# Modulation columns placed behind the MLP's output tiles, the beginning's columns in free slots, the first low halves on VectorE

## The chip, the cores and the metric

The kernel runs on one core of a Trainium2 chip. The metric is the device time of one execution in microseconds (us); the number given is the median of several runs. A core has five engines that each work through their own instructions in order and wait for each other by semaphores: TensorE (PE; its weight loads are the rows PEld), VectorE (DVE), ScalarE (ACT), GpSimd (POOL) and SyncE (SP), whose queue issues all the transfers between main memory and the on-chip memory here. TensorE's results land in PSUM, in banks of 128x512 numbers; everything else lies in SBUF.

## The reference

The program is a decoder trunk of two layers on 512 positions of width 1024, float32 throughout. Each layer has a mixer (an mLSTM of four heads beside a convolution with 31 taps) and a squared-ReLU MLP, and both are modulated by numbers that depend on the vector `c` alone:

```python
c_act = jax.nn.silu(c)
for l in range(DEPTH):                       # DEPTH = 2
    mod = c_act @ w_ada[l] + b_ada[l]        # 1024 -> 6 * 1024
    sh_mix, sc_mix, gt_mix, sh_mlp, sc_mlp, gt_mlp = split(mod, 6)

    h = rms_norm(x, g_pre_mix[l]) * (1 + sc_mix) + sh_mix
    y = mixer(h, ...)                        # w_in, conv, q/k/v, heads, w_out
    x = x + gt_mix * rms_norm(y, g_post_mix[l])

    h = rms_norm(x, g_pre_mlp[l]) * (1 + sc_mlp) + sh_mlp
    f = square(relu(h @ w_ff1[l])) @ w_ff2[l]     # 1024 -> 4096 -> 1024
    x = x + gt_mlp * rms_norm(f, g_post_mlp[l])
```

The change concerns `mod`: 6 x 1024 numbers for each layer, 48 columns of 128, and a weight matrix of 24 MB for each layer that is read once.

## The kernel before

Activations lie with the channels on the 128 partitions and the 512 positions along the row, so x is eight tiles of 128x512. Every large product is computed in three passes of a rounded format (lines 172 to 178): weights and activations are each split into a high half (rounded) and a low half (the rest), and a product is high x high + high x low + low x high. A block of weights of 128x1024 is therefore fetched by SP into one of four `raw` tiles, ScalarE writes its high half (L168) and GpSimd its low half (L169), into two `whi` and two `wlo` tiles, or, where a block is prepared early, into tiles of the pool `slot`, which has 25 (`wblock`, L157). A tile of a product takes 24 passes for each block and ends in one of three `ps_mm` banks.

The modulation is computed in two ways:

- `ada_rows` (L230) on TensorE, for 40 of layer 0's 48 columns, four columns a call: four blocks of 128x1024 of `in_wadn` are fetched into the three `adr` tiles in turn, multiplied by `c` (L239), copied to SBUF (L242), turned to columns by four small products (L244), and VectorE adds the bias (L250, L252). The calls 0 and 2, then 1 and 3, stand at the program's beginning, since the first `h` needs them; the calls 4 to 9 stand among the mixer's steps.
- `ada_col` (L256) on VectorE, for the last 8 columns of layer 0 and the 48 of layer 1: a block of 128x1024 of `in_wadt` is fetched into an `adr` tile and one instruction (L263) multiplies it by the broadcast `c` and sums along the row. The 56 calls stand in the code of layer 0's MLP, one behind each output tile of the first matrix from the eighth on, two behind each of the second (`some`, L280).

The order in which an engine gets its instructions is not that of the code. A scheduler walks through a simulated timeline and places an instruction as early as its inputs, its buffers and its engine are free, weights with a priority ahead of the rest. `behind(later, earlier)` (L105) adds no wait on the chip; it only says that `later` must not be placed ahead of `earlier`.

The beginning (L794 to L813): x comes in, its row sums are formed, the calls 0 and 2 give shift and scale of the first four channel tiles, `make_h` (L333) forms their h with a multiply on VectorE (L338), the high half on ScalarE (L344) and the low half on VectorE (L345), and the same with calls 1 and 3 for the other four. The first six output tiles (`glu_start`, L453) are accumulated side by side in six banks over the eight channel tiles, with weights `in_win0` of 128x768 for each, whose halves lie in slots; the first four channel tiles are called the first half below, the others the second half.

The mixer follows a list of steps (`ORDERS`, L66). The convolution (L416) runs on VectorE as 31 multiply-adds for each of eight channel groups. The heads come in three steps: `head_a` (scores, L649, weighted by VectorE, L651), `head_b` (numerator, L661; then on VectorE statistics L667 and L668, small vectors L670 to L676, a power on GpSimd L146, L679, and the scaling L681) and `head_c` (transposes on TensorE, L690, and the output gate L692, whose halves are split on ScalarE and GpSimd). Between them lie tiles of the output projection (L743). The MLP forms 2 x 16 tiles of the first matrix, each evicted by `f_out` (L753: ScalarE, VectorE L756, ScalarE, VectorE L758), and 2 x 8 tiles of the second, copied by ScalarE (L784) or added by VectorE (L787); `finish` (L347) does the last part of each product with norm and residual.

Of the kernel before, what the change touches and what calls it, by code (L numbers as in the profile page):

```python
# [10 lines left out]
F32 = mybir.dt.float32  # L11
F32R = mybir.dt.float32r
AF = mybir.ActivationFunctionType
ALU = mybir.AluOpType
# [39 lines left out]
def trunk(ctx, tc, xT, vecs, bg, cst, ccol, crow, wadn, wadt, win, win0, wqkv, wgate, wout, wff1, wff2, yT):  # L54
# [174 lines left out]

    def ada_rows(nb, tag):  # L230

        bk = bank(tag)
        for kk in range(NF // 2):
            raw = wpool.tile([P, D], F32, name="adr", tag="adr", bufs=ADR)
            sp.dma_start(out=raw, in_=wadn[nb, kk])
            for j in range(2):
                k = 2 * kk + j
                g = k % 4
                pe.matmul(bk[32 * g:32 * g + 32, :], cc[:, k:k + 1].broadcast_to([P, 32]), raw[:, j * T:(j + 1) * T],  # L239
                          start=(k < 4), stop=(k >= 4), skip_group_check=True)  # L240
# [12 lines left out]

    late = []

    def ada_col(l, c):  # L256

        one, gain = ADA[c // 8]
        scale = 1.0 if gain is None else vec(gain, l)[:, c % 8:c % 8 + 1]
        raw = wpool.tile([P, D], F32, name="adr", tag="adr", bufs=ADR)  # L260
        sp.dma_start(out=raw, in_=wadt[l, c])
        m, ini = mods[l][:, c:c + 1], inits[l][:, c:c + 1]
        dve.tensor_tensor_reduce(raw, raw, cbc, scale, 0.0 if one else ini, ALU.mult, ALU.add, m)  # L263
        if one:
            late.append((l, c))
# [486 lines left out]
    def mlp(l, hp, pre):  # L752
        def f_out(o, pr, ts):  # L753
            rl = scr.tile([P, T], F32, name="rl", tag="rl", bufs=3)
            act.activation(out=rl[:, ts], in_=o, func=AF.Relu)  # L755
            dve.tensor_tensor(o, rl[:, ts], o, op=ALU.mult)  # L756
            act.copy(out=r32(pr[:, 0, ts]), in_=o)  # L757
            dve.tensor_tensor(r32(pr[:, 1, ts]), o, pr[:, 0, ts], op=ALU.subtract)  # L758

        y = None  # L760
        for hf in range(2):
# [19 lines left out]
            for m in range(NF):  # L781
                o = gemm([wff2[l, hf, m, k] for k in range(2 - hf)], fp)
                if hf == 0:
                    act.copy(out=y[m], in_=o)  # L784
                    some(2)
                else:
                    dve.tensor_tensor(y[m], y[m], o, op=ALU.add)  # L787
                    some(2)
# [18 lines left out]
    for hf in range(2):  # L807
        ada_rows(hf, "ax" if hf else "mm")
        ada_rows(2 + hf, "ax" if hf else "mm")
        for i in range(4 * hf, 4 * hf + 4):  # L810
            pre[i] = wblock(win0[i], slot, pri=0)
            hp.append(slot())
# [72 lines left out]
```

## Time and profile before

| | |
|---|---|
| median of 3 runs | 1661.32 us (1660.44 to 1661.95) |
| the profiled execution | 1659.15 us, of it 1657.2 us in the span of the trace |
| TensorE busy | 1568.1 us (95%), 8076 matmuls |
| VectorE busy | 877.9 us (53%) |
| ScalarE busy | 712.7 us (43%) |
| GpSimd busy | 836.0 us (50%) |
| transfers | 188.91 MB, 114 GB/s over the span |

The profile is one execution of the kernel. A row of the timeline gives start, duration, engine, line, operation, the tiles written and read, and in brackets how long the engine had been idle before and what ended that idle time. A row of the table by stretches gives for each engine the busy time and the number of instructions, then the mean clock granted to TensorE (1 is full speed, and it falls to 0.5), the busy share of the DMA engines and what they moved. The row of a group has count, total and mean time. Busy time on TensorE includes work at a lowered clock.

### The profile page before, as it was taken

What the parts mean: (1) busy time and instruction counts of PE and PEld (TensorE: products, weight loads), DVE (VectorE), ACT (ScalarE), POOL (GpSimd) and SP (SyncE); (2) the same over time, 40 slices, a digit from 0 to 9 for tenths busy, and PEclk for the clock granted to TensorE, in tenths of its full rate; (3) what the DMA queues carried; (4) which work ended last, traced back from release to release, by engine and by line L of the source; (5) the groups of instructions that cost most, each with busy time, mean ns of one, the idle gap of its engine ahead of it and who ended that gap; (6) DMA issues with size and microseconds to landing.
All of it is one profiled execution on the core that took longest, in us unless ns stands there. A gap on an engine that the chain in (4) does not pass through costs nothing.

```text
span 1657.2 us, 21339 instructions
## 1 busy us (share of the span) xinstructions
PE 1568.1 (95%) x8076; PEld 1271.7 (77%) x8076; DVE 877.9 (53%) x1685; ACT 712.7 (43%) x1242; POOL 836.0 (50%) x502
## 2 busy tenths in 40 slices
PE   5999989977899999999999999899999999999997
PEld 2677766655699888888899877577789888888887
DVE  2599999799855320022126999988424520012214
ACT  3245664523255432233345367544455432233332
POOL 2557663226584444444555587533585344444462
PEclk7999999988999999999999999999999999999999
DMA  7424333576752232232432022221143132323341
GB/s 282 168 83 139 104 113 127 176 252 217 273 173 63 90 91 100 89 102 89 128 127 84 26 83 81 85 73 55 39 140 103 43 111 89 101 90 96 95 127 52
DMA packets 56270, 188.91 MB, mean 114 GB/s; under 512 B 6376, under 2 KB 8552, under 8 KB 56168
## 3 DMA queue, kind: packets, MB, share of 16 engines
q1 hardware_dynamic: 56168, 187.56, 34.4%
q8 instruction: 63, 1.03, 0.3%
q14 instruction: 39, 0.32, 0.1%
HBM read 185.44 MB, written 2.10 MB: 113 GB/s over the span
## 4 chain that ended last, share of the span: by engine, by line
PE 66%; DVE 12%; POOL 2%; issue 2%; ACT 1%; DMA 1%; POOLq 0%; ACTq 0%; DVEq 0%
PE ps_mm L176 20%; PE ps_mm L177 20%; PE ps_mm L178 20%; DVE ps_cv L416 5%; DVE adr L263 2%; PE ps_mm L661 1%; PE ps_mm L649 1%; DMA adr<-in_wadt 1%; PE ps_ax L303 1%; POOL slot L169 1%; DVE small L477 0%; POOL yt L169 0%; DVE slot L681 0%; ACT whi L168 0%; POOL wlo L169 0%
## 5 line engine op out<-in xcount | busy, mean ns | idle before, releaser
L169 POOL TENSOR_TENSOR wlo<-raw,whi 128x1024 fp32r<-128x1024 f32 (+1 forms) x216 | 499.7, 2314 | 546.8 <-ACT whi L168 518.6
L176 PE MATMUL ps_mm<-slot,whi 128*128 128x512 f32 (+1 forms) x1632 | 626.1, 384 | 10.9 <-ACT slot L154 5.6
L178 PE MATMUL ps_mm<-slot,wlo 128*128 128x512 f32 (+1 forms) x1632 | 623.4, 383 | 1.7 <-POOL wlo L169 1.2
L177 PE MATMUL ps_mm<-slot,whi 128*128 128x512 f32 (+1 forms) x1632 | 624.7, 383 | 0.1
L168 ACT CAST whi<-raw 128x1024 fp32r<-128x1024 f32 (+1 forms) x216 | 216.4, 1002 | 495.4 <-PE ps_mm L177 348.6
L176 PEld LDWEIGHTS ps_mm<-slot,whi 128*128 128x128 f32 x1632 | 309.7, 190 | 80.5 <-ACT slot L154 6.5
L178 PEld LDWEIGHTS ps_mm<-slot,wlo 128*128 128x128 f32 x1632 | 309.7, 190 | 71.8 <-issue 6.2
L177 PEld LDWEIGHTS ps_mm<-slot,whi 128*128 128x128 f32 x1632 | 310.0, 190 | 66.6 <-issue 3.8
L416 DVE SCALAR_TENSOR_TENSOR ps_cv<-slot,vv,ps_cv 128x512 f32<-128x512 f32 x480 | 334.0, 746 | 2.2
L756 DVE TENSOR_TENSOR ps_mm<-rl,ps_mm 128x512 f32<-128x512 f32 (+1 forms) x78 | 46.7, 599 | 390.3 <-ACT rl L755 390.3
L176 PE MATMUL ps_mm<-slot 128*128 128x256 f32 (+1 forms) x568 | 160.5, 293 | 10.1 <-DVE slot L758 7.4
L177 PE MATMUL ps_mm<-slot 128*128 128x256 f32 (+1 forms) x568 | 163.4, 291 | 0.3 <-DVE slot L345 0.3
L178 PE MATMUL ps_mm<-slot 128*128 128x256 f32 (+1 forms) x568 | 162.6, 290 | 0.0
L169 POOL TENSOR_TENSOR slot<-raw,slot 128x1024 fp32r<-128x1024 f32 (+1 forms) x42 | 101.3, 2429 | 58.4 <-ACT slot L168 21.0
L176 PEld LDWEIGHTS ps_mm<-slot 128*128 128x128 f32 x568 | 106.6, 192 | 14.3 <-DVE slot L758 8.3
L177 PEld LDWEIGHTS ps_mm<-slot 128*128 128x128 f32 x568 | 108.5, 191 | 3.5 <-DVE slot L345 1.0
L178 PEld LDWEIGHTS ps_mm<-slot 128*128 128x128 f32 x568 | 108.6, 192 | 1.1
L146 POOL TENSOR_TENSOR small<-small,mhalf 128x4 f32<-128x4 f32 (+1 forms) x38 | 37.4, 983 | 81.8 <-DVE small L145 80.2
L263 DVE CUSTOM_DVE_ANT_0 adr<-adr,cbc,ini 128x1024 f32<-128x1024 f32 x40 | 67.6, 1697 | 8.2 <-DMA adr<-in_wadt 8.2
L519 POOL TENSOR_TENSOR xa<-xa,s 128x512 f32<-128x512 f32 x48 | 62.2, 1295 | 8.9 <-ACT s L518 5.1
L758 DVE TENSOR_TENSOR slot<-ps_mm,slot 128x512 fp32r<-128x512 f32 (+1 forms) x78 | 46.4, 594 | 38.2 <-ACT slot L757 37.9
L757 ACT CAST slot<-ps_mm 128x512 fp32r<-128x512 f32 (+1 forms) x78 | 39.8, 510 | 45.9 <-DVE ps_mm L756 45.9
(202 smaller groups left out, 1643.3 us busy)
## 6 DMA issues: line engine op xcount, KB each, us to landing
raw<-in_wff SPq DMA_DIRECT2D x138, 512.0 KB, 3.5
raw<-in_win SPq DMA_DIRECT2D x58, 512.0 KB, 3.3
adr<-in_wadt SPq DMA_DIRECT2D x56, 512.0 KB, 4.3
adr<-in_wadn SPq DMA_DIRECT2D x40, 512.0 KB, 4.5
raw<-in_wout SPq DMA_DIRECT2D x36, 512.0 KB, 3.6
raw<-in_wqkv SPq DMA_DIRECT2D x24, 256.0 KB, 2.6
raw<-in_win SPq DMA_DIRECT2D x8, 384.0 KB, 7.8
x<-in_xT SPq DMA_DIRECT2D x8, 256.0 KB, 4.8
```

What stands on the lines that cost most here:

```text
L146: pool.tensor_tensor(y, u, mhalf[:, 0:n], op=ALU.pow)
L168: act.copy(out=r32(hi), in_=raw)
L169: (lo_eng or pool).tensor_tensor(r32(lo), raw, hi, op=ALU.subtract)
L176: pe.matmul(out, whi, xh, start=first, stop=False)
L177: pe.matmul(out, whi, xl, start=False, stop=False)
L178: mark[0] = pe.matmul(out, wlo, xh, start=False, stop=last)
L263: dve.tensor_tensor_reduce(raw, raw, cbc, scale, 0.0 if one else ini, ALU.mult, ALU.add, m)
L416: dve.scalar_tensor_tensor(acc, at[i][:, k:k + T], w, acc, op0=ALU.mult, op1=ALU.add)
L519: pool.tensor_tensor(acc, acc, tk, op=ALU.add)
L756: dve.tensor_tensor(o, rl[:, ts], o, op=ALU.mult)
L757: act.copy(out=r32(pr[:, 0, ts]), in_=o)
L758: dve.tensor_tensor(r32(pr[:, 1, ts]), o, pr[:, 0, ts], op=ALU.subtract)
```

## The change

Three things change. The reduction of every column by `ada_col` is placed behind the eviction of the output tile it stands next to in the code: `last[0]` holds the last VectorE instruction of `f_out`, the copy by ScalarE or the addition by VectorE of the second matrix's tile. The column blocks of the calls 0, 2 and 1 of `ada_rows` go to tiles of the pool `slot` in place of the three `adr` tiles (call 3 keeps those). And the low halves of the eight weight blocks `in_win0` are subtracted on VectorE in place of GpSimd.

```diff
--- before.py
+++ after.py
@@ -227,11 +227,14 @@
                 dve.scalar_tensor_tensor(inits[l][:, k], vec("b_ada", l)[:, k], one, vec(gain, l),
                                          op0=ALU.add, op1=ALU.mult)
 
-    def ada_rows(nb, tag):
+    def ada_rows(nb, tag, alloc=None):
 
         bk = bank(tag)
         for kk in range(NF // 2):
-            raw = wpool.tile([P, D], F32, name="adr", tag="adr", bufs=ADR)
+            if alloc is not None and nb < 3:
+                raw = alloc().rearrange("p a b -> p (a b)")
+            else:
+                raw = wpool.tile([P, D], F32, name="adr", tag="adr", bufs=ADR)
             sp.dma_start(out=raw, in_=wadn[nb, kk])
             for j in range(2):
                 k = 2 * kk + j
@@ -251,7 +254,7 @@
             src = m
         dve.tensor_tensor(m, src, inits[0][:, k], op=ALU.add)
 
-    late = []
+    late, last = [], [None]
 
     def ada_col(l, c):
 
@@ -260,7 +263,8 @@
         raw = wpool.tile([P, D], F32, name="adr", tag="adr", bufs=ADR)
         sp.dma_start(out=raw, in_=wadt[l, c])
         m, ini = mods[l][:, c:c + 1], inits[l][:, c:c + 1]
-        dve.tensor_tensor_reduce(raw, raw, cbc, scale, 0.0 if one else ini, ALU.mult, ALU.add, m)
+        red = dve.tensor_tensor_reduce(raw, raw, cbc, scale, 0.0 if one else ini, ALU.mult, ALU.add, m)
+        behind(red, last[0])
         if one:
             late.append((l, c))
 
@@ -755,7 +759,7 @@
             act.activation(out=rl[:, ts], in_=o, func=AF.Relu)
             dve.tensor_tensor(o, rl[:, ts], o, op=ALU.mult)
             act.copy(out=r32(pr[:, 0, ts]), in_=o)
-            dve.tensor_tensor(r32(pr[:, 1, ts]), o, pr[:, 0, ts], op=ALU.subtract)
+            last[0] = dve.tensor_tensor(r32(pr[:, 1, ts]), o, pr[:, 0, ts], op=ALU.subtract)
 
         y = None
         for hf in range(2):
@@ -781,10 +785,10 @@
             for m in range(NF):
                 o = gemm([wff2[l, hf, m, k] for k in range(2 - hf)], fp)
                 if hf == 0:
-                    act.copy(out=y[m], in_=o)
+                    last[0] = act.copy(out=y[m], in_=o)
                     some(2)
                 else:
-                    dve.tensor_tensor(y[m], y[m], o, op=ALU.add)
+                    last[0] = dve.tensor_tensor(y[m], y[m], o, op=ALU.add)
                     some(2)
         some(len(todo))
         ada_bias()
@@ -805,10 +809,10 @@
         pe.matmul(bc0[:, c * P:(c + 1) * P], r0[:, c:c + 1].broadcast_to([P, P]), ident, start=True, stop=True)
     hp, pre = [], {}
     for hf in range(2):
-        ada_rows(hf, "ax" if hf else "mm")
-        ada_rows(2 + hf, "ax" if hf else "mm")
+        ada_rows(hf, "ax" if hf else "mm", slot)
+        ada_rows(2 + hf, "ax" if hf else "mm", slot)
         for i in range(4 * hf, 4 * hf + 4):
-            pre[i] = wblock(win0[i], slot, pri=0)
+            pre[i] = wblock(win0[i], slot, dve, 0)
             hp.append(slot())
             make_h(0, i, x[i], bc0, slice(0, T), hp[i], 8, 0)
     sp.dma_start(out=bgt, in_=bg)
```

The scheduler turns this into other orders; the rows below are instructions of one engine in the order in which they are issued. Lines in the changed kernel are 3 or 4 higher: L266 is the reduction L263, L242 the column product L239.

VectorE at the end of layer 0's mixer, the third head's small vectors (`small`, read with `em`) up to the scaling of its numerator (`slot`), among the fourth head's scores (`s_...`). Before:

```order
L671 TENSOR_TENSOR small<-small,em 128x4
L641 SCALAR_TENSOR_TENSOR s_3107<-ps_ax,cols,cs 128x128
L263 ISA adr,mod_105<-adr,cbc,ini_107,vv 128x1024
L263 ISA mod_105 128x1
L673 RECIPROCAL small<-small 128x4
L263 ISA adr,mod_105<-adr,cbc,ini_107,vv 128x1024
L263 ISA mod_105 128x1
L641 SCALAR_TENSOR_TENSOR s_3116<-ps_ax,cols,cs 128x128
L675 TENSOR_TENSOR small<-small 128x4
L651 SCALAR_TENSOR_TENSOR s_3097<-ps_mm,s_3097 128x512
```

Now, the same place, and behind it the place in the MLP where the first reductions stand:

```order
L672 BN_AGGR small<-small 128x2
L675 TENSOR_TENSOR small<-small,em 128x4
L677 RECIPROCAL small<-small 128x4
L645 SCALAR_TENSOR_TENSOR s_3116<-ps_ax,cols,cs 128x128
L679 TENSOR_TENSOR small<-small 128x4
L680 TENSOR_TENSOR small<-small 128x4
L145 TENSOR_SCALAR small<-small 128x4
L645 SCALAR_TENSOR_TENSOR s_3124<-ps_ax,cols,cs 128x128
L655 SCALAR_TENSOR_TENSOR s_3097<-ps_mm,s_3097 128x512
L683 TENSOR_TENSOR small<-small 128x4
```

```order
L760 TENSOR_TENSOR ps_mm<-rl,ps_mm 128x512
L762 TENSOR_TENSOR slot<-ps_mm,slot 128x512
L266 ISA adr,mod_104<-adr,cbc,ini_106,vv 128x1024
L266 ISA mod_104 128x1
L760 TENSOR_TENSOR ps_mm<-rl,ps_mm 128x512
```

The reductions have left the mixer; the first stands behind the eighth tile of the MLP's first matrix, and the other 55 follow it.

SP's queue in the beginning, behind the transfers of x and the two tables, before (the numbers tell apart tiles of one name):

```order
L235 DMA adr_187<-in_wadn 128x1024
L167 DMA raw_227<-in_win0 128x768
L167 DMA raw_238<-in_win0 128x768
L167 DMA raw_249<-in_win0 128x768
L167 DMA raw_260<-in_win0 128x768
L814 DMA bgt_75<-in_bg 4x4
L575 DMA gw_383<-in_wgate 128x768
L235 DMA adr_191<-in_wadn 128x1024
L235 DMA adr_203<-in_wadn 128x1024
L235 DMA adr_207<-in_wadn 128x1024
L167 DMA raw_320<-in_win0 128x768
```

And now:

```order
L238 DMA slot_211<-in_wadn 128x1024
L238 DMA slot_215<-in_wadn 128x1024
L167 DMA raw_227<-in_win0 128x768
L167 DMA raw_238<-in_win0 128x768
L167 DMA raw_249<-in_win0 128x768
L167 DMA raw_260<-in_win0 128x768
L238 DMA adr_296<-in_wadn 128x1024
L238 DMA adr_300<-in_wadn 128x1024
L238 DMA adr_304<-in_wadn 128x1024
L818 DMA bgt_75<-in_bg 4x4
L579 DMA gw_383<-in_wgate 128x768
L167 DMA raw_320<-in_win0 128x768
```

Before, three column blocks went out, and the fourth waited behind four weight blocks for an `adr` tile. Now all eight of the calls 0 and 2 go out first (the last two shown), and three of call 3 follow the weights; the four of call 1 come two weight blocks later, after `raw_331`, which needs the tile of `raw_238` and so VectorE's low half of it.

TensorE where the first half ends and the second begins (`slot_326` is the fifth channel tile's h, `ps_ax_295` call 3, `ps_ax_271` call 1). Before:

```order
L177 MATMUL ps_cx_393<-slot_266,slot_261 128x512
L178 MATMUL ps_cx_393<-slot_266,slot_262 128x512
L239 MATMUL ps_ax_295<-adr_308,cc_85 32x512 x2
L244 MATMUL ps_ax_295<-cs_73,s2_312 128x1 x4
L176 MATMUL ps_mm_388<-slot_326,slot_321 128x512
```

And now:

```order
L177 MATMUL ps_cx_393<-slot_266,slot_261 128x512
L178 MATMUL ps_cx_393<-slot_266,slot_262 128x512
L247 MATMUL ps_ax_271<-cs_73,s2_288 128x1 x4
L242 MATMUL ps_ax_295<-adr_296,cc_85 32x512 x2
L242 MATMUL ps_ax_295<-adr_300,cc_85 32x512 x2
L242 MATMUL ps_ax_295<-adr_304,cc_85 32x512 x2
L242 MATMUL ps_ax_295<-adr_308,cc_85 32x512 x2
L247 MATMUL ps_ax_295<-cs_73,s2_312 128x1 x4
L176 MATMUL ps_mm_388<-slot_326,slot_321 128x512
```

All four blocks of call 3 are multiplied between the halves, where only the last was before; `adr_308` takes the tile of `adr_296`.

## Prediction, on record before the changed kernel ran

> **What bounds the kernel now.** First the table of busy time by stretch, for the end of the first mixer, a piece of the first MLP and the end of the second mixer (columns: busy time of PE, PEld, DVE, ACT, POOL with their counts, granted clock, DMA share, GB/s):
>
> ```profile
> 351.90:472.00 120.10, 92.86 (x412) 73.18 (x413) 108.09 (x163) 38.43 (x73) 75.08 (x33) 0.87 0.69 239
> 650.00:700.00 50.00, 50.00 (x217) 40.49 (x216) 0.00 (x0) 11.23 (x14) 21.55 (x9) 1.00 0.29 92
> 1160.00:1230.00 70.00, 67.55 (x304) 53.54 (x305) 25.25 (x70) 33.96 (x66) 44.30 (x27) 0.98 0.21 63
> ```
>
> TensorE sets the time of the MLP (50 of 50 us at full clock, VectorE empty). At the end of the first mixer it does not: of 120 us it stands still for 27.2 and runs at a lowered clock, while VectorE is 90% busy. The groups of line 263 say with what:
>
> ```profile
> L263 DVE CUSTOM_DVE_ANT_0 adr<-adr,cbc,ini x40: 1246/1342/3493, 321.9 to 463.9; 128x1024 f32<-128x1024 f32 x40
> L263 DVE CUSTOM_DVE_ANT_0 adr<-adr,cbc,vv x16: 1267/1344/3419, 362.9 to 443.0; 128x1024 f32<-128x1024 f32 x16
> ```
>
> All 56 column reductions run between 322 and 465 us, ahead of the MLP in whose code they stand. The waits of TensorE in that stretch, and the longest of them on the two engines:
>
> ```profile
> PE ps_ax L690 <- DVE slot L681: 20.5, 3, 9.4
> ...
> 396.87 1.56 PE L649 MATMUL ps_mm<-slot 128*128 128x384 f32 x4
> 407.79 1.09 PE L690 MATMUL ps_ax<-cs,slot 128*128 128x128 f32 x4 [9.37 <-DVE slot L681]
> ...
> 380.94 0.42 DVE L667 BATCH_NORM_STATS2 small<-slot 128x6 f32<-128x256 f32 x1
> 382.08 2.38 DVE L263 CUSTOM_DVE_ANT_0 adr<-adr,cbc,ini 128x1024 f32<-128x1024 f32 x1
> 401.72 1.29 DVE L263 CUSTOM_DVE_ANT_0 adr<-adr,cbc,ini 128x1024 f32<-128x1024 f32 x1 [0.77 <-DMA adr<-in_wadt]
> 405.25 3.36 DVE L681 TENSOR_SCALAR slot<-slot,small 128x256 f32<-128x256 f32 x4
> ```
>
> The head's chain on VectorE (L667 to L681) takes 408.6 - 380.9 = 27.7 us; nine reductions lie in it, the first and the last shown, 1.3 to 2.4 us each and some 16 together. Without them and the 0.77 us of waiting for a transfer it is near 11 us, so it would end at about 392, before TensorE has run out of other matmuls at 398.4.
>
> **Columns behind the MLP's tiles.** The order shows all 56 reductions after the eighth output tile of the first MLP. What this frees is read from the same stretch in slices of 10 us, the ones with idle time or a low clock:
>
> ```profile
> 351.90:362.00 10.10, 2.48 (x6) 1.02 (x6) 9.44 (x17) 2.32 (x6) 5.45 (x3) 0.69 0.75 254
> 362.00:372.00 10.00, 7.30 (x24) 5.81 (x25) 9.70 (x20) 2.33 (x7) 1.61 (x1) 0.63 0.77 249
> 372.00:382.00 10.00, 7.34 (x32) 5.12 (x30) 8.40 (x12) 7.40 (x14) 7.71 (x3) 1.00 0.75 255
> 382.00:392.00 10.00, 9.79 (x32) 6.95 (x33) 10.00 (x19) 2.17 (x9) 10.00 (x7) 0.83 0.60 205
> 392.00:402.00 10.00, 6.42 (x26) 4.39 (x24) 9.23 (x18) 4.16 (x9) 4.95 (x4) 1.00 0.62 203
> 402.00:412.00 10.00, 4.21 (x17) 3.77 (x17) 9.96 (x14) 0.00 (x0) 5.50 (x2) 0.57 0.53 177
> 412.00:422.00 10.00, 10.00 (x42) 8.06 (x41) 6.77 (x9) 2.05 (x3) 2.45 (x2) 0.91 0.86 336
> 442.00:452.00 10.00, 5.95 (x27) 4.33 (x26) 8.97 (x22) 0.64 (x2) 4.34 (x2) 0.96 0.73 258
> 452.00:462.00 10.00, 10.00 (x53) 8.62 (x52) 9.21 (x13) 5.50 (x7) 7.00 (x3) 0.87 0.74 258
> ```
>
> Idle: 7.6 + 2.7 + 2.7 + 0.2 + 3.6 + 5.8 + 0 + 4.0 + 0 = 26.6 us. Clock: a mean of 0.69 is taken as 0.62 of the time at half speed, and work at half speed loses half its busy time: 0.5 x (0.62 x 2.48 + 0.74 x 7.30 + 0.34 x 9.79 + 0.86 x 4.21 + 0.18 x 10.0 + 0.08 x 5.95 + 0.26 x 10.0) = 9.4 us. Together 36. The second mixer (the row above) has the same heads and no reductions: there 2.5 us of 70 are idle and 0.04 x 67.6 x 0.5 = 1.4 lost to the clock. For 120 us at that rate 6 us stay, so the gain is **30 us**. Bounds: 36 if nothing stays; 20.5 if only the three waits on L681 go and the clock stays as it is.
>
> What the 56 reductions and their 56 transfers meet in the MLP:
>
> ```profile
> L168 ACT CAST whi<-raw 128x1024 fp32r<-128x1024 f32 (+1 forms) x216 | 216.4, 1002 | 495.4 <-PE ps_mm L177 348.6
> L169 POOL TENSOR_TENSOR wlo<-raw,whi 128x1024 fp32r<-128x1024 f32 x27 | 64.9, 2403 | 85.7 <-ACT whi L168 85.7
> L169 POOL TENSOR_TENSOR wlo<-raw,whi 128x1024 fp32r<-128x1024 f32 x9 | 26.0, 2893 | 37.2 <-ACT whi L168 33.8 <-PE ps_mm L661 3.4
> ```
>
> The second row is 150 us of the MLP (600 to 750), the third 330 to 460, among reductions. A weight block comes every 150 / 27 = 5.6 us; ScalarE's high half takes 1.0, then GpSimd's low half 2.4, 2.9 beside reductions, so 1.7 us of every block stay free. Tiles of the first matrix carry one reduction, those of the second two. A tile's evictions on VectorE queue behind a reduction of 3.5 us at most; three banks of `ps_mm` leave TensorE two further tiles, 11.2 us. SP's queue alternates a weight and a column; a column waits for the reduction three columns before, which is a tile or more old. DMA is at 92 GB/s there, and 56 x 0.52 MB over some 300 us add about 100; the first table shows 239 at a 0.69 share. Cost **0**, covered by those 1.7 us; bounds 0 and 7 (1.0 + 2.4 + two reductions of 1.25 are 5.9 us, 0.3 late, in the 24 blocks of tiles that carry two).
>
> The Trainium skill, "SBUF — State Buffer", section "Who interferes with whom", says that a VectorE instruction with two SBUF inputs and a GpSimd instruction that reads SBUF exclude each other for the whole instruction. By that rule a low half waits at most 1.25 us for one reduction, and the sum stays as it is; the reduction's spread from 1246 to 3493 ns agrees. Two reductions ahead of one low half are 2.5 us by it, which is the upper bound above and the third rival.
>
> **The beginning.** Its rows in order of time:
>
> ```profile
> 0.00:5.00 5.00, 0.00 (x0) 0.00 (x0) 0.17 (x1) 2.68 (x6) 0.30 (x5) 1.00 0.55 160
> 5.00:10.00 5.00, 0.00 (x0) 0.00 (x0) 2.43 (x5) 3.38 (x11) 2.95 (x4) 1.00 0.98 346
> 10.00:15.00 5.00, 3.92 (x20) 3.69 (x24) 2.61 (x22) 1.25 (x4) 1.58 (x3) 1.00 1.03 420
> 15.00:20.00 5.00, 4.20 (x20) 1.72 (x12) 0.00 (x0) 0.83 (x1) 2.76 (x2) 1.00 1.03 403
> ...
> 16.22 0.83 ACT L168 CAST slot<-raw 128x768 fp32r<-128x768 f32 x1 [4.72 <-DMA raw<-in_win]
> 31.50 1.92 PE L239 MATMUL ps_mm<-adr,cc 128*32 128x512 f32 x4 [2.02 <-DMA adr<-in_wadn]
> 36.47 2.72 DVE L338 SCALAR_TENSOR_TENSOR s<-x,mod,ps_ax 128x512 f32<-128x512 f32 x4
> 39.46 1.65 PE L176 MATMUL ps_mm<-slot 128*128 128x512 f32 x3
> 58.73 4.76 SPq L235 DMA_DIRECT2D adr<-in_wadn  x4
> 62.07 1.05 PE L239 MATMUL ps_ax<-adr,cc 128*32 128x512 f32 x4 [0.46 <-DMA adr<-in_wadn]
> 65.36 2.72 DVE L338 SCALAR_TENSOR_TENSOR s<-x,mod,ps_ax 128x512 f32<-128x512 f32 x4
> 66.92 1.65 PE L176 MATMUL ps_mm<-slot 128*128 128x512 f32 x3 [2.06 <-ACT slot L344]
> 86.50 0.39 PE L176 MATMUL ps_mm<-slot,yt 128*128 128x512 f32 x1
> ```
>
> Transfers fill the DMA at some 405 GB/s, so arrival is a matter of bytes. With the eight first column blocks queued together, x, the two tables and those eight are 2.7 + 4.2 = 6.9 MB; the four rows have moved 6.65 MB by 20.0 us, so the eighth is complete at 20.7, plus 1.1 (the first `raw` stands behind 4.7 MB, x, the tables, three column blocks and itself, through at 15.1, and was used at 16.2): 21.8 us. Its matmuls take 1, the way from there to L338 3.05 (36.47 - 33.42), and the low half now ahead of it on VectorE about 0.95 (128x768; L263's 1246 ns for 1024, scaled). L338 starts at 26.8 instead of 36.5; the first weight products 1.56 us later (66.92 - 65.36), at 28.4 instead of 39.46: 11 us gained.
>
> Most is lost again. The second half's 72 products take 86.50 - 66.92 = 19.6 us from a cold clock, and the first half now meets one too and has four column blocks of 1.05 between: 23.8, so it ends at 52.2 (now 61.6, the start of the 0.46 us of waiting). Only there does TensorE read the first block of the fourth call, which still has three buffers, and the fourth block's transfer waits for that read. The row before it and one block (1.6), 62.07 - 58.73 = 3.3 for the transfer, and 66.92 - 62.07 = 4.85 to the second half: 62.0 instead of 66.9. The second half stays as it is. **5 us** gained, handed on to the convolution on VectorE, which begins with its outputs. Bounds: 0, if the second call's four blocks, queued behind a weight that now waits for VectorE, come late; 10, if the fourth block costs no wait and the clock is warm. The eight low halves on VectorE (0.95 each) are covered by the 4.9 us that TensorE spends on each k (19.6 / 4); uncovered, the first four cost 4.
>
> **Sum.** 30 + 0 + 5 = 35. The profiled execution took 1659.15 us (span 1657.2), 2.2 less than the median of 1661.32: 1659.15 - 35 + 2.2 = **1626**.
>
> **Rivals.**
> 1. The beginning gives nothing: the late fourth block, or the second call's. For it: the 3.3 us and the order. Against it: eleven us of lead. 1631.
> 2. The heads' chains are long by themselves, and only half of 36 us is freed: 1661.3 - 18 - 5 = 1638. For it: GpSimd, in the chain too, is busy for 75 of the 120 us. Against it: the second mixer.
> 3. GpSimd bounds the MLP: reductions and low halves take turns, and TensorE waits for `wlo` in each block. Slower from 35 / 56 = 0.63 us of wait per reduction on; with 3.4 us for a low half that is itself held up, two reductions of 1.3 ahead and 1.0 for ScalarE a block takes 7.0 against 5.6 us, and 56 x 1.4 = 78 give about 1704. Against it: only 24 blocks meet two, and the third row has 2.9, not 3.4.
> 4. The reductions slip back ahead of the MLP: the order excludes it.
>
> **Chances.** Forecast (1617 to 1634) 0.62; rival 1 0.15; rival 2 0.14; rival 3 0.05; rival 4 0.01; more than all terms, through waits not counted, 0.03. Range 1612 to 1643: the sum of the upper bounds, 46, gives 1615, and rival 2 is held. A change below 0.2% (3.3 us) can't be told from none here. Faster: all but rivals 3 and 4 and a small share in which half of each fails: 0.93; same 0.02; slower 0.05.
>
> **What would show it.** Right: L690's waits on L681 below 3 us in sum, TensorE over 96% busy from 330 to 450, L266 only after the first MLP's eighth tile, the conv's first glu at about 79 to 81 instead of 84. Wrong: `wlo` as a releaser of TensorE in the MLP, or idle time in the heads with VectorE idle too.

## The result and the profile after

The changed kernel takes 1613.45 us (median of 4 runs, 1610.59 to 1615.61) against 1661.63 us for the kernel before in the same comparison: a ratio of 0.9709, interval 0.9693 to 0.9726. It is 48.2 us faster; 35.3 were forecast. The time lies in the range on record, near its lower edge of 1612, and below the forecast's own range of 1617 to 1634. The gain is also above 46, the sum of the prediction's upper bounds, so the time lies in the range only by the 3 us that were left below that sum.

The profiled execution took 1615.61 us with a span of 1613.5. Its marks beside those of the kernel before (us from the span's start; the first or last start of a group of instructions, by the line numbers of before; a glu is a gated output tile of the product with `in_win0`, or of its like in the second layer):

| mark | before | after | difference so far |
|---|---|---|---|
| first activation of a glu (L444) | 83.2 | 79.6 | 3.6 |
| first matmul of the heads (L649) | 299.3 | 290.7 | 8.6 |
| first L661 | 315.3 | 306.8 | 8.5 |
| first relu of the MLP (L755) | 518.3 | 468.6 | 49.7 |
| first addition of the MLP's last eight tiles (L787) | 795.0 | 744.7 | 50.3 |
| last activation of a glu, the second mixer's start (L444) | 920.0 | 872.1 | 47.9 |
| end of the span | 1657.2 | 1613.5 | 43.7 |

Most of it lies between the first L661 and the first relu, the end of the first mixer. Both kernels do the same 953 matmuls there, so the two rows of the table by stretches can be set against each other. The kernel before:

```profile
315.30:518.30 203.00, 172.77 (x953) 142.59 (x952) 160.24 (x299) 79.38 (x157) 115.02 (x55) 0.92 0.63 215
```

The changed kernel, over the same work, and over the 120 us for which the prediction named a figure:

```profile
306.80:468.60 161.80, 161.01 (x953) 136.35 (x952) 63.46 (x185) 78.88 (x158) 92.50 (x55) 1.00 0.32 98
330.00:450.00 120.00, 119.21 (x683) 101.47 (x682) 41.77 (x113) 55.83 (x105) 78.16 (x45) 1.00 0.31 91
```

203.0 us became 161.8. Of the 41.2 us, 30.2 - 0.8 = 29.4 are idle time, and 172.77 - 161.01 = 11.8 are matmuls that no longer run at a lowered clock (0.92, now 1.00). TensorE is busy for 119.2 of 120 us, 99%. All that is left of its waits in this stretch:

```profile
PE ps_mm L176 <- ACT slot L667: 0.8, 1, 0.8
```

The 20.5 us of waiting for L681 are gone. The groups of the reductions, which now run from the first MLP's eighth output tile to its end:

```profile
L266 DVE CUSTOM_DVE_ANT_0 adr<-adr,cbc,ini x40: 1274/1335/3421, 519.8 to 788.8; 128x1024 f32<-128x1024 f32 x40
L266 DVE CUSTOM_DVE_ANT_0 adr<-adr,cbc,vv x16: 1275/1285/3420, 597.4 to 762.1; 128x1024 f32<-128x1024 f32 x16
```

The beginning in order of time, TensorE's rows at the two half starts and at the fourth call:

```profile
27.56 1.65 PE L176 MATMUL ps_mm<-slot 128*128 128x512 f32 x3 [2.84 <-ACT slot L348]
...
51.90 0.95 PE L247 MATMUL ps_ax<-cs,s 128*128 128x1 f32 x8
53.17 1.91 PE L242 MATMUL ps_ax<-adr,cc 128*32 128x512 f32 x12 [0.32 <-DVE mod L255]
57.95 1.92 PE L242 MATMUL ps_ax<-adr,cc 128*32 128x512 f32 x4 [2.87 <-DMA adr<-in_wadn]
60.55 1.87 PE L247 MATMUL ps_ax<-cs,s 128*128 128x1 f32 x8 [0.68 <-ACT s L245]
64.57 1.65 PE L176 MATMUL ps_mm<-slot 128*128 128x512 f32 x3 [2.15 <-ACT slot L348]
```

The first half starts at 27.56 (39.46 before) and its products end at 51.9. The fourth call's last block comes at 57.95 after 2.87 us of waiting, its four matmuls take 1.92 us and the eight small ones behind them 1.87, each against 1.05 in the kernel before at full clock, and the second half starts at 64.57. The granted clock is 1.00 from 53.1 to 55.1 us and 0.50 from 57.95 to 64.6.

A part that the forecast did not hold is the stage on VectorE after the beginning, from the first glu to the first matmul of the heads: 216.1 us before, 211.1 after. The rows below leave out its first 5 us, in which TensorE still forms the glus. VectorE is the busier engine in it (206.8 of 211.3 us, TensorE 200.8). The kernel before, the row of the stretch and two groups of small instructions on VectorE:

```profile
88.00:299.30 211.30, 200.80 (x923) 144.27 (x921) 206.77 (x361) 119.76 (x201) 122.17 (x95) 0.98 0.33 113
```

```profile
L477 DVE SCALAR_TENSOR_TENSOR small<-small 128x4 f32<-128x4 f32 x7 | 8.1, 1153 | 0.0
...
L145 DVE TENSOR_SCALAR small<-small 128x4 f32<-128x4 f32 x7 | 4.0, 576 | 0.0
```

The changed kernel:

```profile
84.30:290.70 206.40, 199.18 (x923) 142.70 (x921) 203.82 (x361) 119.48 (x201) 122.48 (x95) 0.98 0.34 116
```

```profile
L481 DVE SCALAR_TENSOR_TENSOR small<-small 128x4 f32<-128x4 f32 x7 | 4.6, 656 | 0.3 <-POOL small L146 0.3
...
L145 DVE TENSOR_SCALAR small<-small 128x4 f32<-128x4 f32 x7 | 1.9, 266 | 0.0
```

The same 14 instructions of 128x4 elements take 12.1 us before and 6.5 after. What stretches them stands in the timeline of the kernel before:

```profile
142.74 2.37 POOL L169 TENSOR_TENSOR wlo<-raw,whi 128x1024 fp32r<-128x1024 f32 x1
...
143.50 1.62 DVE L477 SCALAR_TENSOR_TENSOR small<-small 128x4 f32<-128x4 f32 x1
...
162.67 1.09 POOL L508 TENSOR_TENSOR slot<-xp,slot 128x512 fp32r<-128x512 f32 x1
...
162.91 0.91 DVE L145 TENSOR_SCALAR small<-small 128x4 f32<-128x4 f32 x1
...
163.91 1.02 POOL L146 TENSOR_TENSOR small<-small,mhalf 128x4 f32<-128x4 f32 x1
...
165.75 0.15 DVE L477 SCALAR_TENSOR_TENSOR small<-small 128x4 f32<-128x4 f32 x1
```

L477 starts at 143.50, takes 1.62 us and ends at 145.12; the GpSimd instruction that had started before it ends at 145.11. The L145 at 162.91 ends at 163.82, GpSimd's at 163.76. The L477 at 165.75, with GpSimd's instruction over by 164.93, takes 0.15. In the changed kernel VectorE's instructions of this stage stand in another order, since the scheduler places everything behind a changed beginning anew, and less of the small ones' time falls into GpSimd's. VectorE's other instructions became 2.6 us longer in sum, so its busy time fell by 3.0 us, and its idle time by 2.0: the 5 us. That the 14 instructions make the difference is argued from these sums, not tested alone. In both kernels those of the 14 that took longer than 0.18 us all ended within 0.1 us of a GpSimd instruction that had been under way.

Where time was lost is the end of the MLP, its last eight tiles, where two columns stand behind each tile. Up to the fifth of them the additions still follow one another at 5.6 us; from there on GpSimd also has the low halves of the finish, and the next two additions come 6.7 us apart. VectorE and GpSimd in one of these tiles:

```profile
767.03 2.41 POOL L169 TENSOR_TENSOR slot<-raw,slot 128x1024 fp32r<-128x1024 f32 x1 [1.41 <-PE ps_mm L178]
...
767.67 2.85 DVE L266 CUSTOM_DVE_ANT_0 adr<-adr,cbc,ini 128x1024 f32<-128x1024 f32 x1
...
769.40 3.38 POOL L169 TENSOR_TENSOR wlo<-raw,whi 128x1024 fp32r<-128x1024 f32 x1
...
770.46 3.42 DVE L266 CUSTOM_DVE_ANT_0 adr<-adr,cbc,ini 128x1024 f32<-128x1024 f32 x1
...
773.80 0.68 DVE L791 TENSOR_TENSOR yt<-yt,ps_mm 128x512 f32<-128x512 f32 x1
```

From here on the two take turns: the reduction at 770.46 ends when 1.1 us have passed since GpSimd's 769.40 + 3.38 = 772.78, and GpSimd's instruction had ended 2.26 us after the reduction at 767.67 + 2.85 = 770.52. A reduction and a low half take 3.36 us together and not side by side; two of each are 6.7 us, the distance of the additions at 767.07 and 773.80, where TensorE needs 5.6 for a tile. The Trainium skill, "SBUF — State Buffer", section "Who interferes with whom", has an exclusive lock between a VectorE instruction with two SBUF inputs and a GpSimd one that reads SBUF; the rows agree, by the 1.1 and 2.26 us.

TensorE waits for a low half once in these tiles:

```profile
PE ps_mm L178 <- POOL wlo L169: 2.1, 1, 2.1
```

### The profile page after: what moved, and what is told of

It is laid out like the page before. It is cut to its first block, busy times and chain, and to the rows that moved or that the text cites. A ratio compares the mean times of both kernels' runs of the same rounds, so it can differ in the third digit from the quotient of the medians.

```text
span 1613.5 us, 21372 instructions
## 1 busy us (share of the span) xinstructions
PE 1552.8 (96%) x8076; PEld 1266.8 (79%) x8076; DVE 860.3 (53%) x1693; ACT 712.6 (44%) x1242; POOL 803.4 (50%) x494
## 4 chain that ended last, share of the span: by engine, by line
PE 74%; DVE 13%; ACT 2%; POOL 1%; issue 1%; DMA 0%; POOLq 0%; ACTq 0%; DVEq 0%
PE ps_mm L176 22%; PE ps_mm L178 22%; PE ps_mm L177 22%; DVE ps_cv L420 7%; PE ps_mm L665 2%; PE ps_mm L653 2%; PE ps_ax L307 1%; DVE small L481 1%; POOL wlo L169 1%; PE ps_ax L242 1%; ACT whi L168 0%; DVE small L476 0%; PE ps_ax L694 0%; DVE s L603 0%; PE ps_ax L333 0%
## 5 line engine op out<-in xcount | busy, mean ns | idle before, releaser
L169 POOL TENSOR_TENSOR slot<-raw,slot 128x1024 fp32r<-128x1024 f32 x34 | 86.2, 2553 | 12.9 <-issue 11.2
L266 DVE CUSTOM_DVE_ANT_0 adr<-adr,cbc,ini 128x1024 f32<-128x1024 f32 x40 | 65.5, 1649 | 22.0 <-DMA adr<-in_wadt 21.7
```

Source lines behind the costliest of these rows:

```text
L169: (lo_eng or pool).tensor_tensor(r32(lo), raw, hi, op=ALU.subtract)
L266: red = dve.tensor_tensor_reduce(raw, raw, cbc, scale, 0.0 if one else ini, ALU.mult, ALU.add, m)
```

## The experiments

All ratios are to the kernel before, run on the same chip in the same comparison (its medians there were 1659.46 us for the first four runs below; 1658.75 for the fourth call, the columns done early, the short reductions and half of the columns; 1657.86 for the short transfers, the reductions done twice and both extensions). Times of different comparisons are set against each other by these ratios.

### Part one alone

```diff
+        behind(red, last[0])
```
(with `last[0]` set at the MLP's evictions as in the full change; beginning as before)

> Part one alone: the 56 reductions behind the MLP's tiles, the beginning as before. Theory: the end of the first mixer gains 41 us (203.0 us between the first L661 and the first relu of the MLP become about 162), the end of the MLP gives 4 back, and the 4.9 us that VectorE's stage from 88 to 300 us gained in the full change came from the beginning, so this kernel does not have them: 1661.6 - 37 = about 1624. Rival: those 4.9 us come with the moved reductions: about 1619. That the gain needs the earlier beginning: above 1630.

1617.25 us, ratio 0.9747 (0.9734 to 0.976): 42.2 us faster. The end of the first mixer has the full gain without the earlier beginning:

```profile
309.00:470.80 161.80, 161.01 (x953) 136.20 (x952) 63.47 (x185) 79.09 (x158) 92.43 (x55) 1.00 0.30 98
```

The stage on VectorE took 215.2 us, as in the kernel before, so its 5 us do not come with the moved reductions. The size is the rival's all the same: 42.2 us, where the theory's 1624 is a gain of 37.6 and the rival's 1619 one of 42.6. The theory is right on the place and short on the size. In this profile the stretch from the first of the MLP's last eight additions to the second mixer gives back 5.1 us; against that, the beginning is 4.0 earlier and the MLP's body 2.6 shorter, and both scatter by about as much over the other runs (the beginning by the table below; the MLP's body, from its first relu to the first of these additions, takes 273.5 to 276.7 us). Why the median is that low is not shown.

### The beginning alone

```diff
-        behind(red, last[0])
```
(from the changed kernel)

> The two edits of the beginning together, the reductions where they were. Theory: first glu at about 79.6 instead of 83.2 us (3.6 gained), and the stage from 88 to 300 us, bounded by VectorE, shorter by about 5: about 1653. Rival: the stage's 5 us are luck of alignment or belong to the moved reductions: about 1658. A gain handed on into a stage that waits for the reductions anyway: 1661.

1652.89 us, ratio 0.9953 (0.9939 to 0.9966): 6.6 us faster, where the theory's 1653 is a gain of 8.6 and the first rival's 1658 one of 3.6. The stage on VectorE took 211.2 us, so the theory's 5 us are there. The first glu came at 79.3, but with an unchanged beginning it did so too in part one alone (79.3), so the 3.6 us of the profiles of before and after are not the beginning's: the table below has all of them. TensorE's waits at the end of the first mixer are there again:

```profile
PE ps_ax L693 <- DVE slot L684: 10.7, 3, 6.6
```

### Its two edits apart

```diff
-        behind(red, last[0])
...
-            pre[i] = wblock(win0[i], slot, dve, 0)
+            pre[i] = wblock(win0[i], slot, pri=0)
```
(from the changed kernel: only the slots are left)

> Column blocks of the beginning in slots, low halves still on GpSimd. Theory: the first weight products start early as in the full change, at about 27.6 us, but GpSimd's low halves of 2.0 us each (against 0.95 on VectorE) follow one another; covered by TensorE's 4.9 us per block except at the start: second half's end within 2 us of the full change's 82.8, total about 1655. Rival (the two edits need each other): GpSimd holds the first half back by 4 us or more, and the beginning gains nothing: about 1661.

1655.28 us, ratio 0.9974 (0.9964 to 0.9985). The first weight products start at 27.24, as expected; the low halves on GpSimd hold nothing back (second half at 62.13). The stage on VectorE took 216.4 us: without the full change's order its 5 us are not there. That 4.2 us were gained all the same (the theory had 6.6) is not explained by these marks.

```diff
-            pre[i] = wblock(win0[i], slot, pri=0)
+            pre[i] = wblock(win0[i], slot, dve, 0)
```
(in the kernel before)

> Low halves of the first weights on VectorE, column blocks still in three buffers. Theory: the column blocks set the beginning, so the first weight products stay at about 39.5 us and nothing is gained: 1661, within 2. Rival: GpSimd's low halves held back the beginning, or the alignment of VectorE with GpSimd from 88 us on: 3 to 5 us faster, about 1657.

1657.27 us, ratio 0.9991 (0.9979 to 1.0004): no change that is clear of the scatter, as the theory had it. Stage on VectorE 216.0 us.

### The beginning and the stage behind it, over all runs

The same marks in the profile of every run (us):

| kernel | second half starts | first glu | first glu to first matmul of the heads |
|---|---|---|---|
| before | 66.92 | 83.2 | 216.1 |
| part one alone | 63.92 | 79.3 | 215.2 |
| short reductions in the old place | 61.55 | 77.6 | 216.1 |
| the same, short transfers | 62.58 | 77.9 | 215.3 |
| low halves alone | 65.20 | 80.2 | 216.0 |
| slots alone | 62.13 | 78.0 | 216.4 |
| the full change | 64.57 | 79.6 | 211.1 |
| beginning alone | 63.00 | 79.3 | 211.2 |
| columns done early | 64.60 | 79.8 | 211.1 |
| half of the columns behind | 63.70 | 78.8 | 211.1 |
| reductions twice | 61.52 | 76.8 | 211.4 |
| fourth call in slots | 58.22 | 74.0 | 214.3 |
| fourth call in slots, columns done early | 59.04 | 75.0 | 214.2 |

One and the same beginning, with the same order of instructions on every engine, starts its second half anywhere from 61.6 to 66.9 us. The mean of the first four rows, which share the old beginning, is 63.7, of the five with the new one (the full change to reductions twice) 63.5: no gain of the beginning shows, though in the same runs its first half starts 9 us earlier (27.7 against 36.6 on average). With one profile of each, a gain of 1 or 2 us is not excluded; 5 are not there. The last column does not scatter with it. The lengths are 215 to 216, 211 and 214 us, and they go by the order of VectorE's instructions in this stage: it is one and the same in the first five rows, another one, the same again, in the five rows at 211, and a third in the last two; the slots alone have a fourth. Rows with the same order agree within 0.9 us. The 14 small instructions take 11.8 to 12.2 us in the first order, 6.4 to 6.5 in the second, 8.7 in the third, and 11.0 with the slots alone.

### The fourth call in slots too

```diff
-            if alloc is not None and nb < 3:
+            if alloc is not None:
```
(from the changed kernel)

> The changed kernel with the fourth row call's blocks in slots as well, so that its last transfer no longer waits until TensorE has read the call's first block. Theory (this wait of 2.87 us and the half clock after it are what the beginning still loses): the second half starts at about 59.5 instead of 64.6 us, first glu at about 74.5 instead of 79.6, the end 5 us earlier: 1608 to 1609 against 1613.5. Rival: the blocks are late for other reasons (they stand behind weights in the transfer queue), second half at 63 or later, 1613. The stage from 80 to 291 us, on VectorE, took 211.1 us with this order and 215 to 216 with the others; with yet another order it may move the time by up to 5 us either way, which the trace would tell.

TensorE's rows in order of time:

```profile
51.11 0.95 PE L247 MATMUL ps_ax<-cs,s 128*128 128x1 f32 x8
52.38 1.92 PE L242 MATMUL ps_ax<-slot,cc 128*32 128x512 f32 x16 [0.32 <-DVE mod L255]
55.01 1.05 PE L247 MATMUL ps_ax<-cs,s 128*128 128x1 f32 x8 [0.71 <-ACT s L245]
58.22 1.65 PE L176 MATMUL ps_mm<-slot 128*128 128x512 f32 x3 [2.16 <-ACT slot L348]
```

The sixteen matmuls of the fourth call now run in one row behind the first half, without the wait and at full clock, and the second half starts at 58.22, some 5 us earlier than the mean of 63.5. So the wait for the fourth block, with the half clock behind it, is what takes these 5 us, as the theory had it. In the whole it is not seen: 1613.48 us, ratio 0.9719 (0.9691 to 0.9747), which is the rival's time without its reason. The stage on VectorE got yet another order, 214.3 us instead of 211.1, which took 3 of the 5 back; the rest is within the interval.

### Columns done before the last eight tiles

```diff
                 fp.append(pr)
-                some(1)
+                some(1 + hf)
```
(from the changed kernel)

> The changed kernel with two columns instead of one behind each of the sixteen first-matrix tiles of the MLP's second half, so that none is left for its last eight tiles. Theory (in these, reductions and GpSimd's low halves take turns, 1.28 us becomes 3.42 and 2.40 becomes 3.35, and TensorE waits 4 us for the last low half): the 4 us come back, last tile's addition to first finish in line with the kernel before, 1609.5 against 1613.5. Rival: two reductions in a block of 5.6 us hold up the low halves there, TensorE waits for wlo in those sixteen tiles: no gain, or slower, 1613 to 1625. Second rival: the 4 us come from the following stage's own low halves on GpSimd (three in 10.08 us), and stay: 1613.

1609.61 us, ratio 0.9704 (0.9678 to 0.973). The additions of the last eight tiles on VectorE:

```profile
772.86 0.69 DVE L791 TENSOR_TENSOR yt<-yt,ps_mm 128x512 f32<-128x512 f32 x1 [4.90 <-PE ps_mm L178]
778.45 0.69 DVE L791 TENSOR_TENSOR yt<-yt,ps_mm 128x512 f32<-128x512 f32 x1 [4.90 <-PE ps_mm L178]
785.91 0.69 DVE L791 TENSOR_TENSOR yt<-yt,ps_mm 128x512 f32<-128x512 f32 x1 [6.78 <-PE ps_mm L178]
```

The first seven follow one another at 5.6 us. The eighth comes 7.5 us after the seventh, as it does in the kernel before, where the finish's first products go ahead of it. From the first to the first finish it is 42.0 us, as in the kernel before (41.9); the changed kernel took 45.8. TensorE waits for no low half in the sixteen tiles that now carry two columns. So the place and the cause are the theory's.

From the first of these additions to the first finish, the eight profiled kernels that do no reductions there take 41.8 to 42.0 us. The four that do two for each tile take 45.8 (the full change) or 48.1 (part one alone, fourth call in slots, half of the columns). All four wait once, for 2.1 to 2.2 us, for a low half. In the three at 48.1 the granted clock is 0.5 for 3.4 us right behind this wait (a mean of 0.96 over the stretch); in the full change's profile it stays at 1.00. So these tiles cost 3.9 or 6.2 us, and the upper figure holds a lowered clock.

In the time little of this is seen. By the ratios this kernel is 0.8 us faster than the changed one (0.9704 against 0.9709), and the intervals overlap; the theory's 4 us are not shown by the times. Up to the second mixer's start the profiles also scatter more: 125.0 to 129.1 us without reductions there (mean 126.2), 127.4 to 131.7 with them (mean 129.6).

### Short reductions in the old place

```diff
-        dve.tensor_tensor_reduce(raw, raw, cbc, scale, 0.0 if one else ini, ALU.mult, ALU.add, m)
+        dve.tensor_tensor_reduce(raw[:, 0:64], raw[:, 0:64], cbc[:, 0:64], scale, 0.0 if one else ini, ALU.mult, ALU.add, m)
```
(in the kernel before)

> The kernel before, its reductions in their old place but over 64 of 1024 columns each (960 columns of each modulation product are left out). All 56 transfers and waits stay. Theory (VectorE's time in the heads' chains is what costs): the end of the first mixer falls from 203.0 us between first L661 and first relu to 165 or less, about 1622. Rival (it is the 29 MB of transfers, or the place in the queues): it stays above 190, 1650 or more.

1630.08 us, ratio 0.9836 (0.9805 to 0.9866). First L661 to first relu:

```profile
309.50:482.70 173.20, 164.35 (x953) 137.41 (x952) 106.90 (x299) 79.39 (x158) 92.51 (x55) 0.99 0.71 252
```

173.2 us: of the 41.2 us, 29.8 come back when the reductions are short, and 11.4 do not. The stretch is shorter than the rival's 190 and longer than the theory's 165. The transfers were still all there (252 GB/s). To see whether they are the rest, they were made short too:

```diff
-        sp.dma_start(out=raw, in_=wadt[l, c])
+        sp.dma_start(out=raw[:, 0:64], in_=wadt[l, c][:, 0:64])
```

> As the run with short reductions in the old place, and their transfers also cut to 64 of 1024 columns (960 columns of each modulation product are left out): 32 KB instead of 0.5 MB each. Theory (of the 11.4 us that stayed there, most is the chain standing behind short reductions that wait for their transfers, 34.9 us of VectorE's idle time): first L661 to first relu falls from 173.2 to 166 or less, against 161.8 with no reductions there. Rival (56 more instruction pairs on VectorE, taking turns with GpSimd, are the rest): it stays above 170.

1625.83 us, ratio 0.9805 (0.9762 to 0.9847), and the same stretch again takes 173.2 us:

```profile
307.70:480.90 173.20, 165.66 (x953) 138.33 (x952) 88.45 (x299) 79.39 (x158) 92.65 (x55) 0.98 0.32 93
```

At 93 GB/s instead of 252 its length is the same, though the reductions waited for transfers for 13.1 us in sum instead of 34.9 and were all done by 375 us instead of 436. By its own figure that theory fell: the 11.4 us do not go with the transfers. They may still be VectorE's time. The short reductions are not free: they take 44.0 us of it in the first of these two kernels and 25.4 in the second, against 97.8 for the full ones, some of them up to 2.4 us each; and the 16 scalings L681, which end the heads' chains, take 9.6 and 11.5 us there, 5.5 in part one alone. Taking turns with GpSimd would do this, and so might the place of 56 more instruction pairs in the order; which of the two was not settled.

### Half of the columns behind the tiles

```diff
-        behind(red, last[0])
+        if len(todo) < 28:
+            behind(red, last[0])
```
(from the changed kernel)

> The changed kernel with only the second 28 of the 56 reductions held behind the MLP's tiles; the first 28 are free to run in the first mixer's end. Linear theory: half of the 41 us come back, about 1634. Slack theory (VectorE was 90% busy with 56 and would be near 60% with 28; only the excess costs): most of the gain stays, 1613 to 1622. Bunching theory (the 28 run in one row ahead of the first head's chain, which is then as late as before): 1640 or more.

1638.31 us, ratio 0.9877 (0.9856 to 0.9899): near the bunching theory's 1640. First L661 to first relu:

```profile
306.00:494.70 188.70, 172.32 (x953) 144.10 (x952) 111.25 (x242) 78.83 (x157) 101.60 (x55) 0.93 0.49 162
```

188.7 us, so 28 reductions cost 26.9 of the 41.2 us, two thirds. They ran from 315.3 to 385.3, ahead of and within the first heads' chains, and 46.2 us of VectorE's time went into them. The other 28 cost the remaining 14.3. Neither a share of VectorE's time nor its slack gives that: the short reductions above took nearly as much of VectorE's time, 44.0 us, and cost 11.4. Whether it is the first heads' chains in which they stand, or that a stretch already delayed hides more, this run does not tell.

### Reductions done twice

```diff
         behind(red, last[0])
+        dve.tensor_tensor_reduce(raw, raw, cbc, scale, 0.0 if one else ini, ALU.mult, ALU.add, m)
```
(from the changed kernel)

> The changed kernel with each of the 56 reductions done twice on its block (the modulation columns are then products with the square). Theory (reductions and low halves take turns, 2.1 us for a low half and 1.28 for a reduction, and a block of 5.6 us has room for two reductions): nothing until the last eight tiles, whose four reductions and one low half need 7.2 of 5.6 us: 13 us more there, about 1627. Rival (the cover is the 1.7 us that prediction counted for a low half and ScalarE in a row): the sixteen one-block tiles of the second half wait too, 0.3 to 1 us each, 1632 to 1645. Rival (no taking turns: only the reductions themselves get longer): 1613 to 1616.

1630.94 us, ratio 0.9835 (0.9807 to 0.9863). The MLP's body, and its last eight tiles from the first addition to the first finish:

```profile
519.00:745.00 226.00, 226.00 (x975) 182.86 (x974) 156.99 (x215) 72.96 (x97) 101.26 (x41) 1.00 0.57 190
742.50:808.80 66.30, 48.62 (x220) 39.77 (x219) 66.26 (x66) 14.02 (x14) 42.85 (x14) 0.88 0.62 216
```

With twice the reductions, VectorE 157 us busy, TensorE still runs 226 of 226 us up to the last eight tiles; those take 66.3 us instead of 45.8. So the place and the cause are the theory's, and the rival of 1632 to 1645 has no waits to show. The size was 20.5 us and not 13. The theory counted one low half per tile, and from the fourth of these additions on the finish gives GpSimd more; and VectorE's additions themselves come late, from the first of these tiles on (9.7 us to the second). TensorE's waits between 745 and 800 say so; over the whole of the second row they are 15.2 us for the additions and 2.5 for a low half, at a mean clock of 0.88:

```profile
PE ps_mm L176 <- DVE yt L792: 8.2, 2, 7.2
PE ps_mm L178 <- POOL wlo L169: 2.5, 1, 2.5
```

### Both extensions together

The diffs of the fourth call and of the columns done early, on the changed kernel.

> Both extensions together: the fourth row call in slots, and the columns done before the MLP's last eight tiles. By the traces of each alone: second half of the beginning at 58 instead of 64.6 us, of which the stage on VectorE took 3 us back by its other order (214.3 us against 211.1), so about 2.5 us stay; 2.5 to 3 us less from the MLP's last tiles to the next glu (125.9 against 128.9 us on average). Sum 5 to 6 us under the changed kernel, a ratio to the kernel before of 0.967 to 0.969. Rival: the two are not there in the end (each alone was within the interval of the changed kernel): 0.971.

1606.58 us (6 runs, 1603.98 to 1610.99), ratio 0.9689 (0.9662 to 0.9716), in the expected range of 0.967 to 0.969. That is the lowest time of the study and 51 us under the kernel before in its comparison; against the changed kernel's 0.9709 the intervals overlap, so that it is better than that is not shown by times alone. By the marks both waits are gone: second half at 59.0, last eight tiles 42.0 us.

## Why the prediction was right, and where not

**What bounds.** Right. The heads' chains on VectorE were late because of the reductions: with these gone TensorE waits 0.8 us between L661 and the relu, and with short ones in the same place, and all transfers, 72% of the cost is gone. The rival that the chains are long by themselves (1638) is out.

**The 30 us of the first mixer's end.** The mechanism was right and the term too small: 41.2. Two things were mis-sized. The stretch was taken from 351.9 to 472; from the first L661 to the first relu there are 42.0 us of idle time and lowered clock, not 36. And 6 us were held to stay (6.5 by the prediction's own figures), at the rate of the second mixer's stretch, where 0.8 stayed: that stretch has its own waits, and the first mixer, freed, did not have them. The "upper bound" of 36 was none, since it was bounded by the window that had been chosen.

**No cost in the MLP.** Right for its body (no wait of TensorE from 519 to 745 us, and none with twice the reductions). At its end the last eight tiles cost 3.9 us in the full change's profile and 6.2 in three others, within the bound of 7, and by the mechanism that the bound named: reductions and low halves take turns, until TensorE waits. The 6.2 hold 3.4 us at half clock, some 1.7 us lost, which the bound did not have. The bound's "24 blocks of tiles that carry two" was wrong: the eight tiles of the first half have two blocks for two columns and 11.2 us for them. Only the last eight carry two in a block, and what the prediction did not see there are the low halves of the finish, which come on top from the fifth of them on. The third rival's mechanism was real; its price of 78 us was not, because the point from which it decides is reached in the last few tiles only.

**The 5 us of the beginning.** The step failed, though 5 us were gained. The first half came as worked out (27.56 for 28.4, its end 51.9 for 52.2). The second half came at 64.6 and not 62.0. The fourth block was there at 57.95, 0.9 us later than the sum's 57.1; and from there to the second half it took 6.6 us and not 4.85, since TensorE's clock had fallen to half in the wait of 2.87 us, which the sum had left out. The Trainium skill, "TensorE: Matmul & The Clock Gate", section "What's actually happening", says that the clock halves after an idle window; the granted clock of 0.50 and the matmuls of 1.92 us per four behind the wait, against 1.05, agree. The window that the page gives, some 3.4 us, is longer than this wait. The sum was also set against the 66.9 of a single profile, the latest second half of all runs. Over all runs no gain of the beginning shows, which was the first rival. In its place the new beginning came with a new order of VectorE's stage behind it, 5 us shorter, which neither the forecast nor a rival held. That it made up for the missing term is luck.

**The sum.** 35 us were forecast, as 30 and 0 and 5. The two profiled executions differ by 3.6 us in the beginning, which is the chance of two runs, 4.9 in VectorE's stage, 41.2 at the first mixer's end and 0.6 in the MLP's body, less 2.4 at the MLP's end and 4.2 from there to the end of the span, where other runs of the study lie anywhere between 737.0 and 741.5 us: 43.7. The medians differ by 48.2. The profiled execution of before was 2.5 us under its median and that of the changed kernel 2.2 above; which stage the other executions were faster or slower in, no trace shows.

**What was to show it.** The waits on L681 (none left), the 96% (99) and the place of L266 (behind the eighth tile) did. The first glu at 79 to 81 was met (79.6) and told nothing: with the old beginning it lay between 77.6 and 83.2.

## What to carry to other kernels

Compare two kernels over a stretch of equal work (the same count of matmuls between two marks), and take the stretch from mark to mark, not from where the idle time catches the eye; what is left outside it is missing from the sum. Work that nothing waits for soon belongs behind instructions of the engine that has room, and the last tiles before a stage's finish have the least. Before a stage's gain is put down to an edit, look at how far the same stage scatters over runs that did not change it.

## What the runs showed of the hardware that was not expected

A VectorE instruction of 128x4 elements took 0.15 us alone and up to 2.2 us beside a GpSimd instruction (1.62 in the rows shown), ending with it within 0.1 us; 14 of them made 5.6 us of difference in a stage of 211. This holds for a tensor-scalar instruction with one tile read as well (0.91 us at 162.91). A wait of TensorE of 2.1 to 2.2 us in the MLP's last tiles was followed by 3.4 us at half clock in three profiles, which then took 2.3 us more than the fourth, where the clock stayed at 1.00. One and the same beginning differed by up to 5.4 us from run to run in when its second half starts. And with short reductions the end of the first mixer was as long at 252 GB/s of transfers as at 93.
